# Final mLSTM states and forget gates moved in whole rows, and a chunk's decay weights made by one addition and four exponentials, in a one-layer hybrid encoder kernel

## The chip, the cores and the metric

The kernel runs on one core of a Trainium2 chip, in one launch. The metric is the time of the program on the device in microseconds; the time before is the median of three runs. A profiled execution is a run of its own and has its own time. TensorE, VectorE (DVE), ScalarE (ACT), GpSimd (POOL) and SyncE (SP) are the engines; each takes its instructions in the order in which they were laid down, and SP issues nearly all DMAs.

## The reference

One layer is computed for 1024 prompt rows and 32 sample rows with the same weights (D_MODEL 1024). A projection w_in feeds three groups of heads, w_o joins them, and a gated feed-forward network follows; LayerNorms stand between. Cut to what matters here:

```python
# mLSTM, 4 heads of 64 (the kernel: 8 prompt chunks of 128 rows, 1 sample chunk of 32)
dmat    = where(causal, bT[t] - bT[s] + li[s], -inf)
m       = max(m0 + bT, max_s dmat)                 # running stabiliser
s       = (q k^T) * exp(dmat - m)                  # the chunk's weights
num     = s v + (q C0) * exp(m0 + bT - m)
den     = max(|s.sum + (q n0) * exp(m0 + bT - m)|, exp(-m))
h       = num / den
C1, n1  = d0 * C0 + w_end k v^T,  d0 * n0 + w_end k
hm      = head_norm(h) * g * sigmoid(o_gate)
# FoX: 8 heads, causal softmax(q k^T / 8 + F[t] - F[s]) v,  F = cumsum(logf)
# gMLP: LayerNorm, then a causal 128x128 mix of rows per group
mix = concat(hm, hf, hg) @ w_o ;  x = LN(...) ;  y = silu(h w_gate) * (h w_up) @ w_down ;  x = LN(...)
```

Outputs beside y are the keys, values and log forget gates of FoX, the mLSTM states C, n and m of both row groups, and a normalised gMLP value.

## The kernel before, in words

**Layout.** All matrix products are of fp32 numbers split in two fp32r parts, three matmuls each (L118, L119, L120; the row-wise projections L283 to L285, named `tm`). 9060 matmul instructions go out on TensorE. The split is made on the way: ACT casts the high part (L106), DVE or POOL subtracts the low part (L107).

**Stages.** The projections come first (`fm`, `tm`), then attention heads and mLSTM chunks mixed into the rest of the projections and into the feed-forward network of the first row group (`up`, `dn`). ORDER (L42) is a string of units: `q` and `g` make operands, `f` emits a FoX head, `a` a slice of the adaLN product, `m0` to `m3` the first four mLSTM chunks. Chunks 4 to 8 are emitted by `mixers()`, woven with FoX heads 1 to 5. Emission order is not the order on the engines: the framework's scheduler simulates time and places the instructions, with a priority lead (HPA = 200) for FoX and mLSTM. Any change of a buffer or a duration can so move instructions of other parts.

**One chunk** (`mlstm(j)`): loads of q and k (tag `mqk`), of q in block form (`mqb`), v (`mv1`), the output gate (`mo`, L608), the row of maxima (`mb`). ACT makes the sigmoid of `mo` in three passes (L613 to L615). Then the weights `mw`: four DVE instructions (L622), one per head, each max(mb − col, maskbig), and one ACT Exp over all four heads (L624). TensorE multiplies q and k (L627), DVE multiplies the weights in (L629), TensorE multiplies by v (L643) and the old state by q (L648), and DVE adds up `mtot` (L649, L651). L658 and L665 update the state `C`; `C` keeps a head's n as a 65th column beside its 64 columns. The head norm follows (L678 to L696), then `to_mix`: two transposes on TensorE (L706), a copy by ACT (L708) into `mixs` and a store to `dmix` in DRAM.

**Where it is read.** `wo_mix` loads `dmix` back, splits it (L1008/L1009 into `ah`, `al` for the first row group, L1016/L1017 for the second) and the w_o product starts. A gMLP tile has its own way there (`tm_gms`, L740), and FoX heads theirs: scores `fox_s` (L789), maxima on DVE (L793, L796), Exp on ACT (`fox_p`, L798), transposes (`fox_t`, L825), split (`fox_pth` L830 on ACT, `fox_ptl` L831 on DVE), product with v (`fox_o`, L833/L838) and a sum (`fox_fo`, L845). `dn_t` (L933) is a product with ones that gives a LayerNorm's pivot; POOL subtracts it in L1066.

**Buffers.** The tags of the mLSTM pool have one buffer each. `gates()` and the chunks share tags.

Of the kernel before, what the change touches and what calls it, by code (L numbers as in the profile page):

```python
# [15 lines left out]
P = 128  # L16
# [4 lines left out]
NS = 32  # L21
# [48 lines left out]
class Kernel:  # L70
# [365 lines left out]
    def gates(self):  # L436
        self.phase = "gates"
        nc, d = self.nc, self.d
# [24 lines left out]
        scan = t([R, 2, 192], "mqb")  # L463
        nc.gpsimd.memset(scan[:, :, 0:64], NEG)
        scan = [scan[:, 0], scan[:, 1]]
        fk = t([64, 4, P], "mqk", F32R)
        nc.gpsimd.memset(f(fk[:, 2:4, :]), 1.0)
        fq = t([64, 2, P], "mkw", F32R)
        rows4 = t([72, 4, P], "mb")
# [7 lines left out]
        ls, x = x[:, :, 16:28], x[:, :, 0:16]  # L477
        nc.vector.tensor_tensor(x, self.G, self.rowp[:, 0:16].unsqueeze(1).to_broadcast([P, 9, 16]), ALU.add)
        z = x[:, :, 4:16]
        a, e, s, s2 = (y[:, i] for y in (t([P, 2, 9, 12], x) for x in ("mtot", "mhm")) for i in range(2))  # L480
        p = t([P, 9, 12], "msq")
        nc.vector.scalar_tensor_tensor(a, z, -1.0, z, ALU.mult, ALU.min)
        nc.scalar.activation(e, a, AF.Exp)
        nc.vector.tensor_scalar(s, e, 2.0, None, ALU.add)
# [4 lines left out]
        for q in (15, 13, 11, 9, 7, 5, 3):  # L489
# [1 line left out]
        nc.vector.scalar_tensor_tensor(p, p, 1.0, s, ALU.add, ALU.mult)  # L491
        nc.vector.tensor_scalar(a, z, 0.0, None, ALU.min)
        nc.vector.scalar_tensor_tensor(ls, p, -2.0, a, ALU.mult, ALU.add)
        w = t([P, 180], "mixs", F32, 1)
        gi, gm, gn, gf = (w[:, o:o + 9 * n].rearrange("p (j h) -> p j h", h=n)
                          for o, n in ((0, 4), (36, 4), (72, 4), (108, 8)))
        nc.vector.tensor_copy(gf, ls[:, :, 4:12])
        nc.vector.tensor_copy(gi, x[:, :, 0:4])
# [64 lines left out]
        nc.vector.tensor_copy(self.col, ps[:, :4 * R].rearrange("p (g j h) -> p j g h", g=4, h=4))  # L563
        nc.scalar.activation(self.col[:, :, 1:4, :], self.col[:, :, 1:4, :], AF.Exp)
        yield
        self.store(d["o_lf"].rearrange("(j p) h -> p j h", p=P), ls[:, 0:8, 4:12])
        self.store(d["o_lfs"], ls[:NS, 8, 4:12])
        self.store(self.dM, M)
        self.store(d["o_m"], m0[:, 8:9])
        self.store(d["o_ms"], mes)  # L570
# [3 lines left out]
    def mlstm_states(self):  # L574
        nc, d = self.nc, self.d
        self.C = self.t(self.cst, [P, 2, 130], F32, "C")
        self.Cs = self.t(self.cst, [P, 2, 130], F32, "Cs")
        for x in (self.C, self.Cs):
            nc.gpsimd.memset(x, 0.0)
        for i in range(2):  # L580
            r = slice(64 * i, 64 * i + 64)
            self.load(self.Cs[r, :, 65 * i:65 * i + 64], d["state_C"][r])
            self.load(self.Cs[r, :, 65 * i + 64:65 * i + 65], d["state_n"][r].unsqueeze(2))
        self.d0c = self.t(self.cst, [P, 2, 9], F32, "d0c")
        for i in range(2):
            src = self.dd0.rearrange("(a two) j -> two a j", two=2)[i]
            self.load(self.d0c[64 * i:64 * i + 64], src.partition_broadcast(64))
        nc.scalar.activation(self.d0c, self.d0c, AF.Exp)

    def mlstm(self, j):  # L590
# [3 lines left out]
        C = self.C if j < 8 else self.Cs  # L594
        o = j * P
        t = lambda shape, tag, bufs=1: self.t(mx, shape, F32, tag, bufs)
        qk = t([P, 4, P], "mqk", 1)
        self.load(qk[:, :, :L], self.dmqk[:, :, o:o + L])
        qb = t([P, 2, 2, P], "mqb")
        nc.gpsimd.memset(qb, 0.0)  # L600
# [17 lines left out]
        self.phase = "mlstm"  # L618

        w = t([P, 4, P], "mw")  # L620
        for h in range(4):
            nc.vector.scalar_tensor_tensor(w[:L, h, :L], mb[:L, h, :L], col[:L, 0, h:h + 1],  # L622
                                           self.maskbig[:L, :L], ALU.subtract, ALU.max)
        nc.scalar.activation(w[:L, :, :L], w[:L, :, :L], AF.Exp, scale=-1.0)  # L624
        st = self.t(self.pss, [P, 512], F32, "s")
        for i in range(2):
            nc.tensor.matmul(st[:L, 256 * i:256 * i + 256].rearrange("p (a q) -> p a q", a=2)[:, :, :L],  # L627
# [38 lines left out]
                else:  # L666
                    nc.vector.tensor_copy(C[r, i, q], s)
        if j >= 7:
            oc, on = ("o_C", "o_n") if j == 7 else ("o_Cs", "o_ns")
            for a in range(2):  # L670
                r = slice(64 * a, 64 * a + 64)
                self.store(self.d[oc][r], C[r, :, 65 * a:65 * a + 64])
                self.store(self.d[on][r].unsqueeze(2), C[r, :, 65 * a + 64:65 * a + 65])
        yield
        self.phase = "mlstm"

# [8 lines left out]
        nc.vector.tensor_reduce(mu[:L], hm[:L], AX.X, ALU.add)  # L685
        nc.vector.tensor_scalar(mu[:L], mu[:L], 1.0 / 64, None, ALU.mult)
        nc.vector.tensor_tensor(hm[:L], hm[:L], bc(mu), ALU.subtract)
        sq = t([P, 4, 64], "msq")
        nc.scalar.activation(sq[:L], hm[:L], AF.Square)
        var = t([P, 4], "mvar")  # L690
        nc.vector.tensor_reduce(var[:L], sq[:L], AX.X, ALU.add)
# [9 lines left out]
    def to_mix(self, x, j, L, k0, pool, bank=None):  # L701

        nc = self.nc
        ps = bank or self.t(self.pt, [P, 512], F32, "t")
        for i in range(2):
            nc.tensor.transpose(ps[:, i * P:i * P + L], x[:L, i * P:(i + 1) * P], self.ident[:L, :L])  # L706
        s = self.t(pool, [P, 2, P], F32, "mixs", 1)
        nc.scalar.copy(s[:, :, :L], ps[:, :256].rearrange("p (i q) -> p i q", i=2)[:, :, :L])  # L708
        c = min(j // 4, 1)
        o = j * P - GO[c]  # L710
        self.store(self.dmix[c][:, k0:k0 + 2, o:o + L], s[:, :, :L])
# [876 lines left out]
def build(tc, d):  # L1588
# [4 lines left out]

_OUTS = {
    "o_yT": (8, 128, 1056), "o_kT": (8, 64, 1056), "o_v": (1024, 512), "o_vs": (32, 512),
    "o_lf": (1024, 8), "o_lfs": (32, 8), "o_C": (128, 2, 64), "o_n": (128, 2), "o_m": (4, 1),
    "o_Cs": (128, 2, 64), "o_ns": (128, 2), "o_ms": (4, 1), "o_vn": (32, 256),
}


def _layout(inputs):
    import numpy as np

    g = {k: np.asarray(v) for k, v in inputs.items()}
# [31 lines left out]
    qk = np.stack([fq.reshape(1024, 8, 64), fk.reshape(1024, 8, 64)], axis=2).reshape(1024, 1024)  # L1636
    a["w_in"] = units(np.concatenate([mq, mv, mo, gv, gu], axis=1), 256)
    a["w_in_f"] = units(np.concatenate([mk, qk], axis=1), 128)
    a["w_o"] = units(g["w_o"][0], 128)
    a["w_gu"] = np.concatenate([units(g["w_gate"][0], 128), units(g["w_up"][0], 128)], axis=-1)  # L1640
    a["w_dn"] = units(g["w_down"][0], 256)
    a["wsT"] = g["gmlp_ws"][0].transpose(2, 0, 1)
    a["cache_k"] = g["cache_fox_k"][0, 0].transpose(2, 1, 0)
    a["cache_v"] = g["cache_fox_v"][0, 0].reshape(2, 128, 512).transpose(1, 0, 2)
    a["cache_lf"] = g["cache_fox_logf"][0, 0].reshape(2, 128, 8).transpose(1, 0, 2)
    a["state_C"] = g["state_mlstm_C"][0, 0].reshape(2, 128, 64).transpose(1, 0, 2)
    a["state_n"] = g["state_mlstm_n"][0, 0].reshape(2, 128).T
    a["state_m"] = g["state_mlstm_m"][0, 0].reshape(4, 1)
    return {k: np.ascontiguousarray(v) for k, v in a.items()}


def _collect(r):
    import numpy as np

    y = r["o_yT"].reshape(1024, 1056).T
    k = r["o_kT"].transpose(2, 0, 1)
    v = r["o_v"].reshape(1, 1, 1024, 8, 64)

    def state(C, n, m):
        return (C.transpose(1, 0, 2).reshape(1, 1, 4, 64, 64), n.T.reshape(1, 1, 4, 64), m.reshape(1, 1, 4))  # L1660

    out = (y[None, :1024], y[None, 1024:], k[None, None, :1024], v, r["o_lf"].reshape(1, 1, 1024, 8),
           *state(r["o_C"], r["o_n"], r["o_m"]),
           k[None, None, 1024:], r["o_vs"].reshape(1, 1, 32, 8, 64), r["o_lfs"].reshape(1, 1, 32, 8),
           *state(r["o_Cs"], r["o_ns"], r["o_ms"]), r["o_vn"].reshape(1, 1, 32, 256))
    return tuple(np.ascontiguousarray(z) for z in out)


# [20 lines left out]
```

## Time and profile before

| | us |
|---|---|
| median of 3 runs | 1373.39 (1373.31 to 1374.2) |
| profiled execution | 1378.6, span 1376.5 |
| TensorE busy | 1335.4 (97%) |
| TensorE weight loads | 1215.7 (88%) |
| DVE busy | 998.5 (73%) |
| ACT busy | 653.3 (47%) |
| POOL busy | 225.2 (16%) |
| mean granted TensorE clock | 0.995 |

"Idle" of TensorE is time in which no matmul ran; a row of waits gives an engine and a line, what it waited for, the sum, the number of times and the longest. A row of the timeline gives start and duration, the engine and the line, the operation, and in brackets how long the engine stood before it and for whom. In the windows each engine's busy time stands in its column, with the granted clock, the DMA share and GB/s at the end.

### The profile page before, as it was taken

The page shows a single profiled execution, that of the slowest core. Times are in us where ns is not written, and L with a number is a line of the kernel's source. Part 1 is how long each engine was busy: PE and PEld are TensorE (multiplying, and loading weights), DVE is VectorE, ACT ScalarE, POOL GpSimd, SP SyncE. Part 2 cuts the span into 40 slices and gives each one's busy share as a digit, 9 for nine tenths or more (in the row PEclk, how much of TensorE's full clock was granted, in tenths as well). Part 3 has the DMA queues.
Part 4 walks back from the last instruction along what each step waited for, and adds up shares of the span by engine and source line. Part 5 has one row for each costly group of instructions (what it writes and reads, how often), then busy time and mean ns, then how long its engine had stood idle before and what let it go on. Part 6 is the DMA issues. An engine that isn't in the chain of part 4 may idle for free.

```text
span 1376.5 us, 25170 instructions
## 1 busy us (share of the span) xinstructions
PE 1335.4 (97%) x9434; PEld 1215.7 (88%) x9434; DVE 998.5 (73%) x2156; ACT 653.3 (47%) x1282; POOL 225.2 (16%) x259
## 2 busy tenths in 40 slices
PE   7999999999999999999999999999999999999996
PEld 4898889888899768888887889899999999999995
DVE  5545553688769557777766767778898988888777
ACT  3314444444536544545454355436564554545354
POOL 0202000043243200000000000374610000000341
PEclk9999999999999999999999999999999999999998
DMA  9765565545734765543444353564587768454321
GB/s 359 252 241 151 158 198 154 162 146 173 230 114 147 204 176 162 137 143 110 140 128 87 101 120 97 189 169 126 173 226 194 201 161 223 132 175 126 96 87 65
DMA packets 121450, 221.50 MB, mean 161 GB/s; under 512 B 21133, under 2 KB 64537, under 8 KB 121329
## 3 DMA queue, kind: packets, MB, share of 16 engines
q1 hardware_dynamic: 114000, 207.34, 49.0%
q0 software_dynamic: 5968, 11.80, 5.0%
q8 instruction: 74, 1.21, 0.4%
q10 hardware_dynamic: 1360, 0.76, 0.2%
q14 instruction: 48, 0.39, 0.1%
HBM read 188.07 MB, written 51.72 MB: 174 GB/s over the span
## 4 chain that ended last, share of the span: by engine, by line
PE 63%; DMA 5%; DVE 5%; ACT 1%; issue 1%; SPq 0%; ACTq 0%; DVEq 0%
PE up_g L118 5%; PE up_g L120 5%; PE up_g L119 5%; PE dn_g L118 4%; PE dn_g L120 4%; PE dn_g L119 4%; PE sup_u L120 3%; PE sup_u L118 3%; PE sup_u L119 3%; PE sup_g L119 2%; PE sup_g L120 2%; PE sup_g L118 2%; PE wo_g L118 2%; PE dn_u L118 2%; PE wo_g L120 2%; PE dn_u L119 2%
## 5 line engine op out<-in xcount | busy, mean ns | idle before, releaser
L118 PE MATMUL up_g<-mlstm_ah,up_whi 128*128 128x512 f32 (+1 forms) x384 | 141.3, 368 | 2.4 <-DVE up_sil L1147 1.4
L120 PE MATMUL up_g<-mlstm_ah,up_wlo 128*128 128x512 f32 (+1 forms) x384 | 140.6, 366 | 0.0
L119 PE MATMUL up_g<-mlstm_al,up_whi 128*128 128x512 f32 (+1 forms) x384 | 140.5, 366 | 0.0
L1216 ACT CAST sup_whi<-sup_raw 128x1024 fp32r<-128x1024 f32 x54 | 56.0, 1048 | 90.1 <-PE dn_u L119 46.0
L118 PEld LDWEIGHTS up_g<-mlstm_ah,up_whi 128*128 128x128 f32 x384 | 72.6, 189 | 14.6 <-DVE up_sil L1147 1.6
L120 PEld LDWEIGHTS up_g<-mlstm_ah,up_wlo 128*128 128x128 f32 x384 | 72.6, 189 | 11.4
L107 DVE TENSOR_TENSOR up_wlo<-up_raw,up_whi 128x1024 fp32r<-128x1024 f32 x50 | 65.0, 1301 | 23.8 <-ACT up_whi L106 23.3
L106 ACT CAST up_whi<-up_raw 128x1024 fp32r<-128x1024 f32 x50 | 52.4, 1048 | 62.9 <-PE up_g L119 17.5
L119 PEld LDWEIGHTS up_g<-mlstm_al,up_whi 128*128 128x128 f32 x384 | 72.6, 189 | 10.8
L798 ACT ACTIVATE fox_p<-fox_s,fox_fmx 128x384 f32<-128x384 f32 (+2 forms) x96 | 55.2, 579 | 47.0 <-DVE fox_fmx L796 37.2
L1217 DVE TENSOR_TENSOR sup_wlo<-sup_raw,sup_whi 128x1024 fp32r<-128x1024 f32 x54 | 68.0, 1263 | 10.7 <-ACT sup_whi L1216 10.7
L120 PE MATMUL dn_g<-up_acth,dn_wlo 128*128 128x512 f32 (+2 forms) x200 | 73.6, 368 | 0.0
L119 PE MATMUL dn_g<-up_actl,dn_whi 128*128 128x512 f32 (+2 forms) x200 | 73.4, 368 | 0.0
L118 PE MATMUL dn_g<-up_acth,dn_whi 128*128 128x512 f32 (+2 forms) x200 | 73.4, 368 | 0.0
L1071 DVE SCALAR_TENSOR_TENSOR wo_z<-dn_g,start_mod,wo_z 128x512 f32<-128x512 f32 (+4 forms) x120 | 60.3, 521 | 13.4 <-PE dn_g L120 13.0
L106 ACT CAST dn_whi<-dn_raw 128x1024 fp32r<-128x1024 f32 (+1 forms) x44 | 42.7, 971 | 49.9 <-PE dn_u L119 11.1
L830 ACT CAST fox_pth<-fox_t 128x512 fp32r<-128x512 f32 (+1 forms) x80 | 41.0, 544 | 51.9 <-PE fox_t L825 51.8
L831 DVE TENSOR_TENSOR fox_ptl<-fox_t,fox_pth 128x512 fp32r<-128x512 f32 (+1 forms) x80 | 49.5, 631 | 16.7 <-ACT fox_pth L830 16.5
L107 DVE TENSOR_TENSOR dn_wlo<-dn_raw,dn_whi 128x1024 fp32r<-128x1024 f32 (+1 forms) x44 | 49.5, 1126 | 15.8 <-ACT dn_whi L106 15.5
L793 DVE TENSOR_REDUCE fox_fmx<-fox_s 128x1 f32<-128x384 f32 (+2 forms) x96 | 52.7, 553 | 10.1 <-PE fox_s L790 9.1
L283 PE MATMUL tm_g<-tm_whi,start_ah 128*128 128x256 f32 (+1 forms) x192 | 55.1, 290 | 0.0
L283 PE MATMUL tm_g<-tm_whi,start_h1h 128*128 128x256 f32 (+1 forms) x192 | 54.8, 286 | 0.3 <-DVE tm_traw L353 0.2
(668 smaller groups left out, 4813.3 us busy)
## 6 DMA issues: line engine op xcount, KB each, us to landing
up_raw<-w_gu SPq DMA_DIRECT2D x50, 512.0 KB
dn_raw<-w_dn SPq DMA_DIRECT2D x28, 512.0 KB
ada_late<-w_ada SPq DMA_DIRECT2D x24, 512.0 KB
sup_raw<-w_gu SPq DMA_DIRECT2D x20, 512.0 KB
start_dp<-w_gu SPq DMA_DIRECT2D x19, 512.0 KB
start_dp<-w_gu POOLq DMA_DIRECT2D x19, 512.0 KB, 7.5
wo_raw<-w_o SPq DMA_DIRECT2D x18, 512.0 KB
sup_raw<-start_dp SPq DMA_DIRECT2D x18, 512.0 KB
```

The source lines that it names most:

```text
L106: nc.scalar.copy(hi[:, :w], raw[:, :w])
L107: (eng or nc.vector).tensor_tensor(lo[:, :w], raw[:, :w], f(hi[:, :w]), ALU.subtract)
L118: nc.tensor.matmul(ps, hi, xh(k), start=start and k == 0, stop=False)
L119: nc.tensor.matmul(ps, hi, xl(k), start=False, stop=False)
L120: nc.tensor.matmul(ps, lo, xh(k), start=False, stop=stop and k == n - 1)
L283: nc.tensor.matmul(ps[:, :ncol], xh, hi, start=k == 0, stop=False)
L793: nc.vector.tensor_reduce(mxs[:, x:x + 1], s[:, :w], AX.X, ALU.max, negate=True)
L798: nc.scalar.activation(pr[:, lo:hi], banks[x][:, :hi - lo], AF.Exp, bias=mxs[:, 0:1], accum_out=sums[:, x:x + 1])
L831: nc.vector.tensor_tensor(pl[:, :e], ps[:, :e], f(ph[:, :e]), ALU.subtract)
L1071: self.lastz = self.nc.vector.scalar_tensor_tensor(z[:, m, x:y], ps[:, x - a:y - a], g[i], z[:, m, x:y], ALU.mult, ALU.add)
L1216: nc.scalar.copy(h, x)
L1217: tt(l, x, f(h), ALU.subtract)
```

## The change

Four edits. (1) The final states `o_C` and `o_n` (and `o_Cs`, `o_ns`) leave in one store each of the whole state tile, 128 rows of 260 floats, in place of four stores (two of 64-float pieces, two of single floats). The initial state comes in by one such load, so its tile is no longer zeroed by POOL. The host cuts the blocks out. (2) The log forget gates leave as one store of 72 floats a row from the tile `gw`, in place of two stores of 8-float pieces. (3) A chunk's weights: one DVE addition mb + maskbig of 128x512 (L617 after), and four ACT Exps of 128x128 with col as the bias (L620 after). (4) `mqk` has two buffers. For the room, tag `msq` and tag `mixs` are dropped: the squares of the head norm and the result of `to_mix` now lie in `mtot`, and temporaries of `gates()` in other tags. So the next chunk's `mtot` waits until the store to `dmix` has read it. The counts: DVE 2158 to 2131 instructions, ACT 1199 to 1226, POOL 264 to 263, SP 712 to 702, TensorE as before.

```diff
-        fk = t([64, 4, P], "mqk", F32R)
+        fk = t([64, 4, P], "mqk", F32R, 2)
...
-        a, e, s, s2 = (y[:, i] for y in (t([P, 2, 9, 12], x) for x in ("mtot", "mhm")) for i in range(2))
-        p = t([P, 9, 12], "msq")
+        y = t([P, 4, 9, 12], "p", F32, 4)
+        a, e, s, s2 = (y[:, i] for i in range(4))
+        p = t([P, 9, 12], "mtot")
...
-        self.store(d["o_lf"].rearrange("(j p) h -> p j h", p=P), ls[:, 0:8, 4:12])
-        self.store(d["o_lfs"], ls[:NS, 8, 4:12])
+        self.store(d["o_lf"], gw[:, 108:180])
...
-        for x in (self.C, self.Cs):
-            nc.gpsimd.memset(x, 0.0)
-        for i in range(2):
-            r = slice(64 * i, 64 * i + 64)
-            self.load(self.Cs[r, :, 65 * i:65 * i + 64], d["state_C"][r])
-            self.load(self.Cs[r, :, 65 * i + 64:65 * i + 65], d["state_n"][r].unsqueeze(2))
+        nc.gpsimd.memset(self.C, 0.0)
+        self.load(self.Cs, d["state_C"])
...
-        qk = t([P, 4, P], "mqk", 1)
+        qk = t([P, 4, P], "mqk", 2)
...
+        nc.vector.tensor_tensor(w[:L, :, :L], mb[:L, :, :L],
+                                self.maskbig[:L, :L].unsqueeze(1).to_broadcast([L, 4, L]), ALU.add)
         for h in range(4):
-            nc.vector.scalar_tensor_tensor(w[:L, h, :L], mb[:L, h, :L], col[:L, 0, h:h + 1],
-                                           self.maskbig[:L, :L], ALU.subtract, ALU.max)
-        nc.scalar.activation(w[:L, :, :L], w[:L, :, :L], AF.Exp, scale=-1.0)
+            nc.scalar.activation(w[:L, h, :L], w[:L, h, :L], AF.Exp, bias=col[:L, 0, h:h + 1], scale=-1.0)
...
         if j >= 7:
-            oc, on = ("o_C", "o_n") if j == 7 else ("o_Cs", "o_ns")
-            for a in range(2):
-                r = slice(64 * a, 64 * a + 64)
-                self.store(self.d[oc][r], C[r, :, 65 * a:65 * a + 64])
-                self.store(self.d[on][r].unsqueeze(2), C[r, :, 65 * a + 64:65 * a + 65])
+            self.store(self.d["o_C" if j == 7 else "o_Cs"], C)
...
-        sq = t([P, 4, 64], "msq")
+        sq = t([P, 4, 64], "mtot")
...
-        s = self.t(pool, [P, 2, P], F32, "mixs", 1)
+        s = self.t(pool, [P, 2, P], F32, "mtot", 1)
```

How the order moves on the engines is shown at three places. Line numbers after the change are 4 less at the weights' product (L625 for L629) and 4 to 8 less behind it.

First SP where chunk 7 ends and chunk 8's output gate is loaded, before:

```order
454 L87 DMA mlstm_mv_1392_7233<-start_dmv_61 32x4x64
455 L91 DMA o_C<-fm_C_2249 128x1x64
456 L91 DMA o_n<-fm_C_2249 128x1x1
457 L91 DMA o_C<-fm_C_2249 128x1x64
458 L91 DMA o_n<-fm_C_2249 128x1x1
459 L87 DMA mlstm_mo_7236<-start_dmo_62 32x256
460 L87 DMA dn_raw_9490<-w_dn 128x1024
461 L87 DMA fox_v_7199<-start_dv_59 128x8x128
```

and after:

```order
451 L87 DMA dn_raw_9410<-w_dn 128x1024
452 L91 DMA o_C<-fm_C_2247 128x260
453 L87 DMA mlstm_mo_7227<-start_dmo_62 32x256
454 L87 DMA dn_raw_9444<-w_dn 128x1024
455 L87 DMA fox_v_7190<-start_dv_59 128x8x128
456 L91 DMA start_dmix_33_89<-mlstm_mtot_7183 128x2x128
```

The load of `mo` still follows the state store directly; four rows became one.

Second DVE between the last step of chunk 1 (`mhm` times `mo`) and the `mtot` of chunk 2, before:

```order
455 L665 SCALAR_TENSOR_TENSOR fm_C_2249<-fm_C_2249,fm_d0c_2257,mlstm_s_3539 64x65 x4
456 L696 TENSOR_TENSOR mlstm_mhm_3550<-mlstm_mhm_3550,mlstm_mo_3505 128x256
457 L733 SCALAR_TENSOR_TENSOR tm_vhl_4136<-tm_g_4111,start_colp_108,tm_vhl_4136 128x2x64 x4
458 L629 TENSOR_TENSOR mlstm_mw_3646<-mlstm_s_3652,mlstm_mw_3646 128x512
459 L637 TENSOR_TENSOR mlstm_mkw_3659<-mlstm_t_3656,start_col_178 128x256
460 L622 SCALAR_TENSOR_TENSOR mlstm_mw_3829<-mlstm_mb_3823,start_col_178,start_maskbig_136 128x128 x4
461 L649 TENSOR_TENSOR mlstm_mtot_3666<-mlstm_s_3667,start_col_178 128x260
```

and after:

```order
456 L688 TENSOR_TENSOR mlstm_mhm_3544<-mlstm_mhm_3544,mlstm_mo_3499 128x256
457 L661 SCALAR_TENSOR_TENSOR fm_C_2247<-fm_C_2247,fm_d0c_2251,mlstm_s_3533 64x65 x4
458 L625 TENSOR_TENSOR mlstm_mw_3640<-mlstm_s_3646,mlstm_mw_3640 128x512
459 L633 TENSOR_TENSOR mlstm_mkw_3653<-mlstm_t_3650,start_col_178 128x256
460 L725 SCALAR_TENSOR_TENSOR tm_vhl_4130<-tm_g_4105,start_colp_108,tm_vhl_4130 128x2x64 x4
461 L617 TENSOR_TENSOR mlstm_mw_3823<-mlstm_mb_3817,start_maskbig_136 128x512
462 L645 TENSOR_TENSOR mlstm_mtot_3660<-mlstm_s_3661,start_col_178 128x260
```

The four subtractions (L622) are one addition (L617), and the state update moved behind the last step of chunk 1. L645 now needs the store of chunk 1's result, which is made from that last step.

Third TensorE where the last FoX head of the second row group ends, before:

```order
4907 L838 MATMUL fox_o_7778<-fox_pth_7822,fox_v_7653 128x256
4908 L833 MATMUL fox_o_7778<-fox_ptl_7823,fox_v_7653 64x256
4909 L838 MATMUL fox_o_7778<-fox_pth_7822,fox_v_7653 128x256
4910 L933 MATMUL dn_t_9926<-wo_z_755_3920,start_ones_45_140 128x512
4911 L119 MATMUL dn_g_10038<-up_actl_9559,dn_whi_10019 128x512
4912 L120 MATMUL dn_g_10038<-up_acth_9558,dn_wlo_10020 128x512
```

and after:

```order
4872 L830 MATMUL fox_o_7766<-fox_pth_7797,fox_v_7641 128x256
4873 L925 MATMUL dn_t_9914<-wo_z_754_3914,start_ones_45_140 128x512
4874 L825 MATMUL fox_o_7766<-fox_ptl_7811,fox_v_7641 64x256
4875 L830 MATMUL fox_o_7766<-fox_pth_7810,fox_v_7641 128x256
4876 L825 MATMUL fox_o_7766<-fox_ptl_7811,fox_v_7641 64x256
4877 L830 MATMUL fox_o_7766<-fox_pth_7810,fox_v_7641 128x256
4878 L119 MATMUL dn_g_9975<-up_actl_9691,dn_whi_9971 128x512
```

The end of the head and the pivot stand some 35 rows earlier. Up to the first w_o product of the second row group (row 5015 before, 5012 after) follow 8 rows of `dn_g` and 96 of `up` before, and 38 of `dn_g` and 96 of `up` after.

More of the change, by code (lines that the diff above doesn't have):

```diff
@@ L493, in gates @@
         nc.vector.scalar_tensor_tensor(ls, p, -2.0, a, ALU.mult, ALU.add)
-        w = t([P, 180], "mixs", F32, 1)
-        gi, gm, gn, gf = (w[:, o:o + 9 * n].rearrange("p (j h) -> p j h", h=n)
+        gw = t([P, 180], "mhm")
+        gi, gm, gn, gf = (gw[:, o:o + 9 * n].rearrange("p (j h) -> p j h", h=n)
                           for o, n in ((0, 4), (36, 4), (72, 4), (108, 8)))
@@ L1595 @@
     "o_yT": (8, 128, 1056), "o_kT": (8, 64, 1056), "o_v": (1024, 512), "o_vs": (32, 512),
-    "o_lf": (1024, 8), "o_lfs": (32, 8), "o_C": (128, 2, 64), "o_n": (128, 2), "o_m": (4, 1),
-    "o_Cs": (128, 2, 64), "o_ns": (128, 2), "o_ms": (4, 1), "o_vn": (32, 256),
+    "o_lf": (128, 72), "o_C": (128, 2, 130), "o_m": (4, 1),
+    "o_Cs": (128, 2, 130), "o_ms": (4, 1), "o_vn": (32, 256),
 }
@@ L1645, in _layout @@
     a["cache_lf"] = g["cache_fox_logf"][0, 0].reshape(2, 128, 8).transpose(1, 0, 2)
-    a["state_C"] = g["state_mlstm_C"][0, 0].reshape(2, 128, 64).transpose(1, 0, 2)
-    a["state_n"] = g["state_mlstm_n"][0, 0].reshape(2, 128).T
+    cn = np.concatenate([g["state_mlstm_C"][0, 0], g["state_mlstm_n"][0, 0][:, :, None]], axis=2)
+    cn = cn.reshape(2, 2, 64, 65).transpose(1, 2, 0, 3)
+    a["state_C"] = np.zeros((128, 2, 130), cn.dtype)
+    for i in range(2):
+        a["state_C"][64 * i:64 * i + 64, :, 65 * i:65 * i + 65] = cn[i]
     a["state_m"] = g["state_mlstm_m"][0, 0].reshape(4, 1)
@@ L1657, in _collect, with state @@
     v = r["o_v"].reshape(1, 1, 1024, 8, 64)
[L1659 to L1665, printed above, removed]
+    def state(C, m):
+        C = np.stack([C[64 * i:64 * i + 64, :, 65 * i:65 * i + 65] for i in range(2)])
+        C = C.transpose(2, 0, 1, 3).reshape(1, 1, 4, 64, 65)
+        return C[..., :64], C[..., 64], m.reshape(1, 1, 4)
+    lf = r["o_lf"].reshape(128, 9, 8).transpose(1, 0, 2)
+    out = (y[None, :1024], y[None, 1024:], k[None, None, :1024], v, lf[None, None, :8].reshape(1, 1, 1024, 8),
+           *state(r["o_C"], r["o_m"]),
+           k[None, None, 1024:], r["o_vs"].reshape(1, 1, 32, 8, 64), lf[8, :32].reshape(1, 1, 32, 8),
+           *state(r["o_Cs"], r["o_ms"]), r["o_vn"].reshape(1, 1, 32, 256))
     return tuple(np.ascontiguousarray(z) for z in out)
```

## The prediction

> **What bounds the kernel now.** I read the page first, then the stretches of 100 us, then what TensorE waited for, then the timeline of the other engines at each of its larger gaps.
>
> ```profile
> span 1376.5 us, 25170 instructions
> PE 1335.4 (97%) x9434; PEld 1215.7 (88%) x9434; DVE 998.5 (73%) x2156; ACT 653.3 (47%) x1282; POOL 225.2 (16%) x259
> ```
>
> TensorE works 1335.4 of 1376.5 us. The change takes no matmul away, so all it can win is in the 41 us of idle time and in time at a lower clock. Some of it is the start and the tail of the kernel. Within, the waits of TensorE show where it lies (total, times, longest):
>
> ```profile
> PE fox_s L789 <- ACT fox_p L798: 4.0, 3, 2.4
> PE wo_g L118 <- ACT up_ah L1016: 2.6, 1, 2.6
> PE fm_g L118 <- ACT tm_gms L740: 2.4, 1, 2.4
> PE mlstm_t L635 <- DVE fox_ptl L831: 2.3, 1, 2.3
> ```
>
> They are gaps of 2.3 to 2.6 us (fox_s has two small ones beside), and each lies where mLSTM chunks, attention heads or the operand of w_o pass from engine to engine. I take them one by one. Everything below is in time of the profiled execution.
>
> **The state stores (gap at 743 us).** The last chunk (j = 8) stands here; SP first stores the final state, then loads that chunk's output gates (mo). Timeline of SP, of ACT and of PE, then the chain of waits, then two stretches of 1 us (the last two columns are DMA share and GB/s):
>
> ```profile
> 728.33 0.60 SPq L91 DMA_DIRECT2D o_n<-fm_C  x1
> ...
> 731.93 0.34 SPq L87 DMA_DIRECT2D mlstm_mo<-start_dmo  x1
> 734.83 0.59 SPq L87 DMA_DIRECT2D fox_v<-start_dv  x1
> 740.59 0.41 ACT L613 ACTIVATE mlstm_mo<-mlstm_mo 32x256 f32<-32x256 f32 x1 [6.62 <-DMA mlstm_mo<-start_dmo]
> 743.07 0.44 PE L789 MATMUL fox_s<-fox_k,fox_qp 128*128 128x384 f32 x1 [2.36 <-ACT fox_p L798]
> 731.93 8.57 DMA mlstm_mo<-start_dmo
> 738.00:739.00 1.00, 1.00 (x6) 0.82 (x5) 0.00 (x0) 0.00 (x0) 0.00 (x0) 1.00 0.67 29
> 742.00:743.00 1.00, 0.00 (x0) 0.00 (x0) 0.57 (x2) 0.97 (x4) 0.00 (x0) 1.00 0.95 334
> ```
>
> A load of 32 KB takes 8.57 us, since almost nothing moves (29 GB/s at 738) until 742, although SP has issued a load of fox_v as well at 734.83. ACT stands in order behind that load at L613 for 6.62 us, fox_p L798 stands behind L613, and TensorE runs dry for 2.36 us. After such a gap the granted clock falls (windows of PE; third figure from the right):
>
> ```profile
> 744.00:746.00 2.00, 2.00 (x8) 0.58 0.50 143
> 746.00:748.00 2.00, 2.00 (x7) 0.56 0.34 37
> ```
>
> That is 2 × 0.42 + 2 × 0.44 = 1.7 us of lost work. The change writes the state as 128 rows of 1,040 B in place of 256 pieces of 256 B and 256 of 4 B, in one DMA instead of four. The price of the new store is not in the trace; its nearest row is the store of a chunk's result, 2.87 us (row below). If mo then lands 2.9 to 3.9 us after its issue at 731.93 (the rows of other transfers below), it is there at 735.8 at the latest, ACT loses at most 1.8 us instead of 6.62, and the 2.36 us are more than covered. **Term: 2.36 + 1.7 = 4.1 us gained**; bounds 0 (the stall is not of the stores) and 4.1. The stores of the last state (o_Cs, o_ns) appear in no wait of TensorE, so they gain nothing. Row then rule: the row above has 8.57 us behind 4 B pieces; the Trainium skill, page "DMA: Bandwidth & Descriptors", section "Specifications", sets 512 B as the least transfer at line rate, with a read-modify-write below that, which points the same way. But its section "Why small descriptors are slow (HBM only)" prices a packet at a fixed 3 cycles or so, and by that alone 512 small pieces would be no stall of microseconds and the term would be 0.
>
> The state loads at the start have the same form; I count nothing for them, since the waits above show no TensorE wait on them.
>
> **The weights of a chunk (gap at 303 us).** Durations of the forms (min/median/max in ns): old subtraction, old Exp, and for what is new the nearest forms, a DVE TENSOR_TENSOR of 128x512 (L629) and an ACT pass of 128x128 (mean in the last place but one):
>
> ```profile
> L622 DVE SCALAR_TENSOR_TENSOR mlstm_mw<-mlstm_mb,start_col,start_maskbig x36: 233/347/3212, 177.8 to 720.6; 128x128 f32<-128x128 f32 x32, 32x32 f32<-32x32 f32 x4
> L624 ACT ACTIVATE mlstm_mw<-mlstm_mw x9: 304/634/647, 178.9 to 721.2; 128x512 f32<-128x512 f32 x8, 32x128 f32<-32x128 f32 x1
> L629 DVE TENSOR_TENSOR mlstm_mw<-mlstm_s,mlstm_mw x9: 270/692/694, 252.1 to 753.5; 128x512 f32<-128x512 f32 x8, 32x128 f32<-32x128 f32 x1
> L798 ACT ACTIVATE fox_p<-fox_s,fox_fmx 128x128 f32<-128x128 f32 x8 | 2.9, 368 | 2.7 <-DVE fox_fmx L793 2.4
> ```
>
> DVE: 4 × 0.347 − 0.692 = 0.70 us less a chunk. ACT: 4 × 0.368 − 0.634 = 0.84 us more. Nine times each, 6 us and 8 us, on engines at 73% and 47%: off the path, except where they set a gap. That is here:
>
> ```profile
> 297.54 4.00 DVE L622 SCALAR_TENSOR_TENSOR mlstm_mw<-mlstm_mb,start_col,start_maskbig 128x128 f32<-128x128 f32 x4
> 297.51 2.40 POOL L107 TENSOR_TENSOR tm_wlo<-tm_raw,tm_whi 128x1024 fp32r<-128x1024 f32 x1
> 301.63 0.63 ACT L624 ACTIVATE mlstm_mw<-mlstm_mw 128x512 f32<-128x512 f32 x1 [3.44 <-DVE mlstm_mw L622]
> 303.45 0.44 PE L635 MATMUL mlstm_t<-start_ident,mlstm_mqk 128*128 128x128 f32 x2 [2.27 <-DVE fox_ptl L831]
> ```
>
> The first of the four subtractions stood behind POOL (its maximum of 3,212 ns), then ACT's Exp, then fox_pth, then fox_ptl, then TensorE. In the new order the one addition stands at the same place behind POOL, with two inputs in SBUF as well. It ends some 0.4 us sooner after the wait, and ACT gives that back with three more Exps ahead of fox_pth. **Term: 0**, bounds −4.0 (the 2.27 us go, and 1.7 us of clock as at 743) and +0.8.
>
> **Order: buffers and the wait that is added.** With two mqk buffers the attention and mLSTM stream stands 20 to 30 TensorE rows earlier. In exchange chunk j+1's tot (L649) shares its one buffer with chunk j's result and must wait for that store to land. DVE waits in order, with fox_ptl, the maxima of fox and the norms of gMLP queued behind it, and TensorE waits for those. Rows at chunk 1 to 2 and chunk 2 to 3, and the landing:
>
> ```profile
> 313.37 0.37 SPq L91 DMA_DIRECT2D start_dmix<-mlstm_mixs  x1
> 314.83 2.06 SPq L87 DMA_DIRECT2D mlstm_mqb<-start_dmqk  x2
> 320.17 0.42 DVE L649 TENSOR_TENSOR mlstm_mtot<-mlstm_s,start_col 128x260 f32<-128x260 f32 x1
> 340.84 0.97 DVE L696 TENSOR_TENSOR mlstm_mhm<-mlstm_mhm,mlstm_mo 128x256 f32<-128x256 f32 x1
> 344.42 0.37 SPq L91 DMA_DIRECT2D start_dmix<-mlstm_mixs  x1
> 357.84 2.87 DMA start_dmix<-mlstm_mixs
> 361.11 3.90 DMA mlstm_al<-start_dmix
> ```
>
> Chunk 1 to 2: the store could land at 313.37 + 2.87 = 316.2, 3.9 us ahead of L649. Now the two mqb loads go ahead of it on SP, so 314.83 + 2.06 + 2.87 + 0.4 = 320.2: it lands as L649 had begun. The wait eats what DVE saves and no more. Chunk 2 to 3: from L696's end (341.81) to the landing (344.42 + 2.87 = 347.29) are 5.5 us. Between these two steps on DVE stand about 6 us of work in the new order. No wait, by a margin of half a microsecond. **Term: 0**, with a bound of 2 us of DVE wait at each place if the store lands 4 us after issue and not 2.87.
>
> The last rows above are also the chain of the gap at 366: m3's store 2.87, the load of al 3.90, two ACT steps, TensorE. In the new order 13 instead of 8 tm matmuls stand between m3's transposes and the work that runs dry, and the chain has for one of them:
>
> ```profile
> 357.06 0.12 PE tm_g L284
> ```
>
> **Term: 5 × 0.12 = 0.6 us gained** of 2.4.
>
> The gap of 2.6 us ahead of wo_g (timelines of DVE and POOL, then two rows of the chain):
>
> ```profile
> 877.94 5.86 DVE L1017 TENSOR_TENSOR up_al<-wo_tmp,up_ah 128x272 fp32r<-128x272 f32 x4
> 873.88 11.06 POOL L1066 TENSOR_TENSOR wo_z<-wo_z,up_pv 128x512 f32<-128x512 f32 x7 [129.30 <-ACT up_pv L934]
> 885.47 1.49 DVE L1017 TENSOR_TENSOR up_al<-wo_tmp,up_ah 128x272 fp32r<-128x272 f32 x4
> 886.61 5.10 DMA wo_tmp<-start_dmix
> 873.18 0.23 PE dn_g L119
> ```
>
> L1017's four take 5.86 us beside POOL's pass against 1.49 us once POOL is done, so the last wo_tmp loads go out late. The last fox_o and the pivot that starts POOL (dn_t) now have 38 instead of 8 dn_g matmuls behind them before w_o: 30 × 0.23 = 7 us more, well over the 2.6. But DVE and SP have their own order there. **Term: 2.0 us gained**, bounds 0 and 2.6.
>
> **Sum.** 4.1 + 0.6 + 2.0 = 6.7 us: 1378.6 − 6.7 = 1371.9 for the profiled execution, whose span is 1376.5. The median of the runs shown is 1373.39, 5.2 us under it; the same difference makes **1366.7 us**.
>
> One rule on the clock bears on the spread. After the gaps of 2.27 us (303) and 2.36 us (743) the clock fell, and after that of 2.4 us at 366 it stayed at 1.00:
>
> ```profile
> 304.00:306.00 2.00, 2.00 (x11) 0.50 0.79 173
> 368.00:370.00 2.00, 2.00 (x20) 1.00 1.06 409
> ```
>
> So length does not decide it here, and any gap that is moved can win or lose 1.7 us. The Trainium skill, page "TensorE: Matmul & The Clock Gate", section "What's actually happening", has a free-running activity window of some 3.4 us: by that, no gap here would be long enough for a full idle window, and the term at 743 would be 2.36 alone. The rows at 744 and 746 speak against that.
>
> **The rivals.** (1) Only the stall at 743 goes; what the order wins at 366 and 892 it loses elsewhere: 1373.39 − 4.1 = 1369.3. For it: 4.1 is the one term with a direct cause. (2) More goes: the 303 gap too (its DVE steps fall past POOL's), and all of 892: 4.1 + 4.0 + 0.6 + 2.6 = 11.3, so 1362.1. Against it: the addition still meets POOL in the order. (3) The change does not do what it says: the 4 B pieces are not what starves mo, or mo's buffer is free later anyway; then only the order's terms are left, 0 to 2.6, and 1371 to 1373.4. For it: no row shows a store of 1,040 B rows by itself. Against it: nothing else stands between o_n and the silence. (4) **Slower:** tot's wait decides. The store of chunk 1 and of chunk 2 lands 2 us after DVE is ready, at the place where DVE is fullest; TensorE runs dry 2 us each and loses 1.7 us of clock each: 7.4 lost, 4.1 gained, 1373.39 + 3.3 = 1376.7. It decides from a landing of some 3.5 us on at chunk 2. For it: al's 3.90 us on the same queue, and SP holds al loads ahead of that store. Against it: TensorE has work from gMLP that does not wait for fox.
>
> **How the numbers follow.** About 0.2% (2.7 us) is what a measurement of this kernel can tell from no change. Chances: forecast 0.42, (1) 0.20, (2) 0.08, (3) 0.13, (4) 0.17. Forecast, (1) and (2) are faster by more than 2.7 us, less 0.03 for a miss inside them: 0.67. Same: (3), those 0.03 and 0.03 of (4) where only one wait falls: 0.19. Slower: 0.14. The range goes from (2)'s 1362.1 to (4)'s 1376.7; most of the chance lies in 1362 to 1370.
>
> **What would show it.** Right: mo's DMA under 4 us, no silence of the DMA engines after o_C, no gap of PE L789 on fox_p near 740, clock 1.00 there; the wait of wo_g on up_ah gone or under 1 us; the wait on tm_gms near 1.8. Wrong: mo still at 8 us; DVE L649 (L645 after) waiting for a DMA of start_dmix; more than 42 us of TensorE idle, or clock windows of 0.5 to 0.8 in new places.

## The result, and the profile after

The changed kernel is faster by 0.2%: median 1372.99 us of 12 runs against 1376.34 of 12 runs of before on the same chips (the first three of these gave the 1373.39 of the table above), ratio 0.9978 with a 95% interval of 0.9968 to 0.9989, or 3.0 us (1.5 to 4.4). The forecast was 6.7 us (ratio 0.9951). The direction was right and the size was not: 3.0 of 6.7 us came. The profiled execution has 1375.06 us against 1378.6, its span 1373.0 against 1376.5.

The page after, two lines:

```profile
span 1373.0 us, 25163 instructions
PE 1332.9 (97%) x9434; PEld 1216.8 (89%) x9434; DVE 989.9 (72%) x2129; ACT 657.5 (48%) x1309; POOL 223.6 (16%) x258
```

TensorE is idle for 40.1 us where it was 41.1: hardly less. But the idle time has moved. Stretches of 100 us of the changed kernel (length, busy time of TensorE, clock, DMA share, GB/s):

```profile
300.00:400.00 100.00, 89.69 (x711) 0.97 0.58 189
700.00:800.00 100.00, 100.00 (x514) 1.00 0.39 117
800.00:900.00 100.00, 100.00 (x628) 1.00 0.41 131
```

and the same of before:

```profile
300.00:400.00 100.00, 93.42 (x753) 0.98 0.61 192
700.00:800.00 100.00, 97.64 (x495) 0.98 0.45 106
800.00:900.00 100.00, 97.44 (x606) 1.00 0.44 135
```

From 700 to 900 TensorE now never stops: 4.9 us of gaps and the low clock behind 743 are gone, as forecast. From 300 to 400 it has lost 3.7 us more. The waits of TensorE after name the losses:

```profile
PE tm_g L722 <- DMA tm_gvn<-start_dvn: 3.0, 1, 3.0
PE fm_g L118 <- ACT tm_gms L732: 3.0, 1, 3.0
PE mlstm_t L631 <- DVE fox_ptl L823: 2.3, 1, 2.3
PE foxs_s L882 <- DMA foxs_k<-start_dsf: 1.8, 1, 1.8
```

The second and third are the gaps of 366 and 303 of before. The first is new: a load of gMLP values from DRAM (tm_gvn) that TensorE needs for L722 (L730 before). The fourth, 0.2 before, was gone in a second execution of the changed kernel.

The two gaps that went. Chunk 8's output gate, SP then ACT of the changed kernel:

```profile
729.92 0.34 SPq L87 DMA_DIRECT2D mlstm_mo<-start_dmo  x1
731.96 0.42 ACT L609 ACTIVATE mlstm_mo<-mlstm_mo 32x256 f32<-32x256 f32 x1 [0.58 <-DMA mlstm_mo<-start_dmo]
```

The load takes 2.0 us where it took 8.57, and ACT stands 0.58 us for it where it stood 6.62. And the operand of the second w_o product, POOL's pivot and ACT's last cast before it:

```profile
865.85 9.03 POOL L1058 TENSOR_TENSOR wo_z<-wo_z,up_pv 128x512 f32<-128x512 f32 x6 [129.63 <-ACT up_pv L926]
889.90 1.64 ACT L1008 CAST up_ah<-wo_tmp 128x272 fp32r<-128x272 f32 x4 [0.67 <-DMA wo_tmp<-start_dmix]
```

POOL starts at 865.85 where it started at 873.88, and the w_o product waits for nothing.

### The profile page after: what moved, and what is told of

Its sections match the earlier page's. It is cut to its first block, busy times and chain, and to the rows that moved or that the text cites. A ratio compares the mean times of both kernels' runs of the same rounds, so it can differ in the third digit from the quotient of the medians.

```text
span 1373.0 us, 25163 instructions
## 1 busy us (share of the span) xinstructions
PE 1332.9 (97%) x9434; PEld 1216.8 (89%) x9434; DVE 989.9 (72%) x2129; ACT 657.5 (48%) x1309; POOL 223.6 (16%) x258
## 4 chain that ended last, share of the span: by engine, by line
PE 81%; DVE 7%; DMA 7%; ACT 2%; issue 2%; SPq 1%; ACTq 0%; DVEq 0%
PE up_g L118 5%; PE up_g L120 5%; PE up_g L119 5%; PE dn_g L118 4%; PE dn_g L120 4%; PE dn_g L119 4%; PE tm_g L284 3%; PE tm_g L283 3%; PE tm_g L285 3%; PE sup_u L120 3%; PE sup_u L118 3%; PE sup_u L119 3%; PE fox_t L817 2%; PE sup_g L119 2%; PE sup_g L120 2%; PE sup_g L118 2%
## 5 line engine op out<-in xcount | busy, mean ns | idle before, releaser
L284 PE MATMUL tm_g<-tm_wlo,start_h1h 128*128 128x256 f32 (+1 forms) x192 | 54.9, 286 | 0.9 <-DVE tm_wlo L107 0.9
```

The costliest lines, as they stand in the source:

```text
L284: nc.tensor.matmul(ps[:, :ncol], xh, lo, start=False, stop=False)
```

## The experiments

Twelve experiments follow, two of them the kernels before and after once more. Ratios are against runs of before on the same chip. A ratio is given where a kernel was timed several times; e6, e7, e9 and e10 are one profiled execution each. The store of the log gates (part 2) and the load of the initial state were not tried by themselves.

### Each part alone, and the change without its buffers (e1 to e4)

e1, the state stores alone:

```diff
-            oc, on = ("o_C", "o_n") if j == 7 else ("o_Cs", "o_ns")
-            for a in range(2): ...  # four stores
+            self.store(self.d["o_C" if j == 7 else "o_Cs"], C)
```

> Before with one edit: o_C/o_n and o_Cs/o_ns leave as one whole-row store each. TensorE's order is that of before, row for row. Theory (the pieces of 256 B and 4 B starve the load of mo): that load lands in under 4 us after its issue instead of 8.57, TensorE's gap of 2.36 us near 743 and the low clock behind it are gone, every other gap stays (303: 2.3, 366: 2.4, 892: 2.6); 4.1 us faster than before. Rival (the order of the changed kernel took that gap away, not the stores): the gap near 743 stays, 0 us.

Ratio 0.9983 (0.9970 to 0.9995), 2.3 us. The gap near 743 is gone:

```profile
734.98 0.33 SPq L87 DMA_DIRECT2D mlstm_mo<-start_dmo  x1
736.93 0.40 ACT L613 ACTIVATE mlstm_mo<-mlstm_mo 32x256 f32<-32x256 f32 x1
```

The load takes 1.95 us at the most. TensorE's order is that of before, so the stores did this and not the order. But the other gaps were not what they had been: the same order waited 1.53 us for tm_gvn (0 in the first profile of before) and 3.0 for tm_gms (2.4). The theory's 4.1 us did not come in full, though the interval (0.7 to 4.1 us) does not shut it out.

e2, two mqk buffers and the tags that make room (the lines of `gates()` are left out here):

```diff
-        qk = t([P, 4, P], "mqk", 1)
+        qk = t([P, 4, P], "mqk", 2)
...
-        sq = t([P, 4, 64], "msq")
+        sq = t([P, 4, 64], "mtot")
...
-        s = self.t(pool, [P, 2, P], F32, "mixs", 1)
+        s = self.t(pool, [P, 2, P], F32, "mtot", 1)
```

> Before with one edit: two mqk buffers and the tags that pay for them (msq, mixs into mtot; gates' temporaries moved). Theory (this part moved the instructions, and the loss between 303 and 376 us is its): a TensorE wait of about 3 us on tm_gvn near 312 and one of about 3 on tm_gms near 366-370, the gap near 743 stays at about 2.4; slower than before by 2 to 6 us. Rival (the weights edit moved the instructions): no wait on tm_gvn over 0.5 us, time within 1.5 us of before.

Ratio 0.9992 (0.9980 to 1.0004): no difference that can be told. No wait on tm_gvn. So the theory, that the loss belongs to this part, fell. Its order has a gap of its own, 3.95 us at 333 for fox_p, and a smaller one (1.30) at 740.

e3, the weights alone:

```diff
-        for h in range(4):
-            nc.vector.scalar_tensor_tensor(w[:L, h, :L], mb[:L, h, :L], col[:L, 0, h:h + 1], ..., ALU.subtract, ALU.max)
-        nc.scalar.activation(w[:L, :, :L], w[:L, :, :L], AF.Exp, scale=-1.0)
+        nc.vector.tensor_tensor(w[:L, :, :L], mb[:L, :, :L], ..., ALU.add)
+        for h in range(4):
+            nc.scalar.activation(w[:L, h, :L], w[:L, h, :L], AF.Exp, bias=col[:L, 0, h:h + 1], scale=-1.0)
```

> Before with one edit: a chunk's weights by one addition and four Exps. Theory (its cost is hidden, and the 303 gap stays, since the one addition waits for POOL like the first of four): the addition near 298 takes 3.4 to 3.7 us, the gap near 303 is 2.2 to 2.3, no wait on tm_gvn over 0.5 us; within 1.5 us of before. Rival (this edit brings the loss): a tm_gvn wait of about 3 us, slower by 2 to 6 us.

Ratio 0.9999 (0.9988 to 1.0010). The rival is right about the wait (1.89 us), but not about the time. The gap at 303 was 2.23 us behind an addition of 3.60, as the theory had it. No gap stood near 743, and larger ones than in before, 1.4 to 1.9 us, stood at 453, 492 and 518. So the gaps moved, and TensorE was idle no less in sum (42.8 us, 41.1 in before). The wait:

```profile
311.28 1.13 PE L730 MATMUL tm_g<-tm_gvn,start_wsp 128*128 128x128 f32 x8 [1.89 <-DMA tm_gvn<-start_dvn]
```

e4, the changed kernel without the buffers of e2 (the lines of e2 the other way round):

> The changed kernel with one mqk buffer and the old tags (parts 1 to 3 of the change alone). Theory (the loss between 303 and 376 comes with the buffers): no tm_gvn wait over 0.5 us, no gap near 743; 4 us faster than before, and 1 us or more faster than the changed kernel. Rival (the loss belongs to any new order): a gap of 2 to 3 us on tm_gvn or elsewhere in 300 to 380 in this order too, no faster than the changed kernel.

Ratio 0.9991 (0.9978 to 1.0005). The rival again: 1.96 us on tm_gvn, 2.69 ahead of the w_o product. No gap near 743.

What follows from the four: a wait of some 2 us on tm_gvn is there with the weights' edit (e3, e4) and is not there with the buffers alone (e2). The wait by itself does not prove it, since e1, in the order of before, had 1.53 us as well; what the edit changes is the order on SP, shown below. And the gap ahead of the second w_o product was 2.6 to 2.75 us in all four, so no part alone takes it away.

### Weights and buffers together (e5)

The diffs of e2 and e3, with the stores of before.

> Before with two edits together: the weights (one addition, four Exps) and the two mqk buffers with their tags; the state and gate stores are those of before. TensorE's order is then that of the changed kernel row for row, with the pivot dn_t 139 matmuls ahead of the second w_o product (105 in before and in either edit alone). Theory (the gap ahead of that product goes by this order): no wait of wo_g on up_ah near 890, where e1 to e4 all had 2.6 to 2.75 us; 2 to 4 us faster than before. Rival (the stores took it away): the gap stays at 2.6.

Ratio 0.9983 (0.9965 to 1.0001). The gap ahead of w_o is gone and the one near 743 is there (1.88 us). Only with both edits does the scheduler put the pivot early; the order alone does it, and the stores have no part in it. The time is 2.3 us under before, with an interval that just reaches no difference. The wait on tm_gvn is there too (1.69 us).

### Which pieces stop the DMAs (e6, e7)

e6 is e1 with the single floats stored as well:

```diff
             self.store(self.d["o_C" if j == 7 else "o_Cs"], C)
+            for a in range(2):
+                r = slice(64 * a, 64 * a + 64)
+                self.store(self.d["o_n" if j == 7 else "o_ns"][r].unsqueeze(2), C[r, :, 65 * a + 64:65 * a + 65])
```

> e1 with the old stores of single floats (o_n, o_ns) added behind the whole-row store, as outputs that nobody reads. TensorE's order is that of before. Theory (the 4 B pieces starve the load of mo): mo lands 7 us or more after its issue, ACT waits 4 us or more for it. Rival (the pieces of 256 B do it): mo lands about 2 us after its issue, as in e1.

e7 stores the state in pieces of 65 floats and no single ones:

```diff
-            self.store(self.d["o_C" if j == 7 else "o_Cs"], C)
+            for a in range(2):
+                r = slice(64 * a, 64 * a + 64)
+                self.store(self.d["o_C" if j == 7 else "o_Cs"][r], C[r, :, 65 * a:65 * a + 65])
```

> e1 with the state stored in two DMAs of 128 pieces of 260 B each (64 columns and n together), no single floats. TensorE's order is that of before. Theory (4 B pieces): mo lands about 2 to 3 us after its issue and ACT does not wait over 1 us for it. Rival (any piece under 512 B): mo lands after 5 us or more.

SP and ACT of e6:

```profile
731.93 0.33 SPq L87 DMA_DIRECT2D mlstm_mo<-start_dmo  x1
739.35 0.42 ACT L613 ACTIVATE mlstm_mo<-mlstm_mo 32x256 f32<-32x256 f32 x1 [5.39 <-DMA mlstm_mo<-start_dmo]
```

and of e7:

```profile
728.36 1.24 SPq L91 DMA_DIRECT2D o_C<-fm_C  x2
732.60 0.34 SPq L87 DMA_DIRECT2D mlstm_mo<-start_dmo  x1
734.53 0.40 ACT L613 ACTIVATE mlstm_mo<-mlstm_mo 32x256 f32<-32x256 f32 x1
```

7.42 us with the single floats, 1.93 us at the most without them. The pieces of 4 B stop the load, and pieces of 260 B do not. Of the rule that the Trainium skill gives on the page "DMA: Bandwidth & Descriptors", section "Specifications" (512 B as the least transfer at line rate), only this much shows here: 4 B were far too small, and 260 B were small enough to be under it and cost mo nothing.

### The gap at 303 (e8)

```diff
-GENG = (0, 1, 1, 0)
+GENG = (0, 0, 0, 0)
```

> The changed kernel with GENG = (0, 0, 0, 0): the low parts of the gMLP weights (four subtractions of 128x1024) on DVE and not on POOL. Theory (the gap near 303 is DVE's addition waiting for POOL's 2.4 us subtraction): the addition near 298 takes 0.7 to 1.5 us instead of 3.6, the gap near 303 falls from 2.25 to under 1, tm_gvn is loaded earlier; 1 to 4 us faster than the changed kernel. Rival (the added 4 x 1.2 us of DVE work in its fullest stretch eat it): the same wait elsewhere between 280 and 350, no faster than the changed kernel.

Ratio 0.9940 (0.9923 to 0.9958), median 1369.04: 8.3 us under before. The addition of the changed kernel, then that of e8 (DVE):

```profile
297.83 3.60 DVE L617 TENSOR_TENSOR mlstm_mw<-mlstm_mb,start_maskbig 128x512 f32<-128x512 f32 x1
295.35 0.88 DVE L617 TENSOR_TENSOR mlstm_mw<-mlstm_mb,start_maskbig 128x512 f32<-128x512 f32 x1
```

Without POOL's subtraction beside it the addition takes 0.88 us instead of 3.60, and the 303 gap and the wait on tm_gvn are both gone. The DVE work that is added shows only as waits of 0.6 to 0.8 us between 316 and 328; tm_gms is waited for once more, 2.93 us at 377.

### The same kernels again (e9, e10)

Before and the changed kernel, each unchanged, a second profiled execution.

> The kernel before, unchanged, a second profiled execution. Theory (the waits on loads between 300 and 380 differ from execution to execution, and the first profile of before had few of them): the gaps near 303 (2.3) and 743 (1 to 2.4, behind a load of mo of 7 us or more) and 890 (2.4 to 2.8) come again; a wait on tm_gvn of 0 to 1.6 us and one on tm_gms of 2 to 3; mean granted clock anywhere in 0.991 to 0.996. Rival (the profile repeats itself to 0.2 us): no wait on tm_gvn, 2.4 on tm_gms.

> The changed kernel, unchanged, a second profiled execution. Theory: the load of a fifth 512 KB piece (tm_raw) stands ahead of tm_gvn in SP's order whatever the execution: tm_gvn lands 9 us or more after its issue, TensorE waits 1.5 to 3 us for it near 311; no gap near 735 or 890; the wait on foxs_k near 484 is 0 to 1.8. Rival (the tm_gvn wait of 3 us was chance): under 0.7 us.

1377.8 us for before, 1371.66 for the changed kernel. In e9 the gap near 743 came again, but only 1.45 us of it, and with no low clock behind it. The clock fell behind 303, as in the first execution, and here also behind the gaps at 366 and 489. There was no wait on tm_gvn. Windows of 2 us:

```profile
304.00:306.00 2.00, 2.00 (x13) 0.63 0.99 295
744.00:746.00 2.00, 1.77 (x10) 1.00 0.58 169
```

In e10 the new wait came again, almost to the hundredth. Chain and TensorE, first of the changed kernel, then of e10:

```profile
303.32 9.15 DMA tm_gvn<-start_dvn
312.60 0.96 PE L722 MATMUL tm_g<-tm_gvn,start_wsp 128*128 128x128 f32 x6 [3.05 <-DMA tm_gvn<-start_dvn]
302.07 9.13 DMA tm_gvn<-start_dvn
311.33 1.62 PE L722 MATMUL tm_g<-tm_gvn,start_wsp 128*128 128x128 f32 x6 [3.03 <-DMA tm_gvn<-start_dvn]
```

So it belongs to the kernel. The wait on tm_gms was 2.32 in e9 and 2.97 in e10, as in the first profiles (2.43 and 2.96).

### The new wait taken away (e11, e12)

SP of the changed kernel shows what stands ahead of tm_gvn:

```profile
301.46 0.33 SPq L87 DMA_DIRECT2D mlstm_mb<-start_dM  x1
301.88 0.38 SPq L87 DMA_DIRECT2D tm_raw<-w_in  x1
302.36 0.86 SPq L87 DMA_DIRECT2D ada_late<-w_ada  x2
303.32 0.46 SPq L87 DMA_DIRECT2D tm_gvn<-start_dvn  x1
```

and of e9 (before again):

```profile
294.27 0.33 SPq L87 DMA_DIRECT2D tm_raw<-w_in  x1
300.31 0.33 SPq L87 DMA_DIRECT2D mlstm_mb<-start_dM  x1
300.74 0.86 SPq L87 DMA_DIRECT2D ada_late<-w_ada  x2
301.70 0.37 SPq L87 DMA_DIRECT2D tm_gvn<-start_dvn  x1
```

mb has one buffer, so chunk 3's can be loaded only when chunk 2's weights are made from the last one, and these stand behind POOL. In before tm_raw (512 KB) was ahead of mb on SP and so went out 6 us earlier. In the changed kernel it stands behind mb, goes out with the two loads of ada_late, and tm_gvn comes after 1.5 MB instead of 1 MB. The weights' edit brings this order: e3, e4 and e5 have it as well, e1, e2, e6 and e7 do not. From tm_gvn's issue to the first matmul that waited for it passed 9.3 to 9.5 us in the five profiles with the new order on SP (e3, e4, e5, the changed kernel, e10) and 7.4 to 7.7 us in the two of the old order in which TensorE waited for it at all (e1 1.53 us, e6 1.22). e11 gives mb a second buffer (and mqk one, for the room):

```diff
-        qk = t([P, 4, P], "mqk", 2)
+        qk = t([P, 4, P], "mqk", 1)
...
-        mb = t([P, 4, P], "mb", 1)
+        mb = t([P, 4, P], "mb", 2)
```

> The changed kernel with two buffers for mb (and one for mqk, since both do not fit): the load of the next chunk's mb no longer waits for the weights' addition, and the load of tm_raw no longer stands behind it on SP. Theory (the tm_gvn wait is that order on SP): tm_raw is issued some 5 us ahead of ada_late, tm_gvn lands 7.3 to 7.9 us after its issue as in before, the wait near 311 is under 1 us; pivot 139 matmuls ahead, so no gap near 890; 1 to 3 us faster than the changed kernel. Rival (the wait comes from TensorE's order): 1.5 us or more near 311.

Ratio 0.9938 (0.9919 to 0.9957), median 1370.01: 8.5 us under before by the ratio, where the changed kernel has 3.0. SP and TensorE of e11:

```profile
295.21 0.34 SPq L87 DMA_DIRECT2D tm_raw<-w_in  x1
298.66 0.92 SPq L87 DMA_DIRECT2D ada_late<-w_ada  x2
300.46 0.33 SPq L87 DMA_DIRECT2D tm_gvn<-start_dvn  x1
309.84 1.05 PE L722 MATMUL tm_g<-tm_gvn,start_wsp 128*128 128x128 f32 x8
```

tm_raw is early again, tm_gvn is not behind mb, and L722 does not wait. (When tm_gvn landed can't be read here, since nothing waited for it.) Over the changed kernel that is 5.5 us by the two ratios, where 1 to 3 were expected; by an estimate from their two intervals it may be 2.5 to 8.5. Its profile also has none of the low clock between 310 and 380 that both profiles of the changed kernel have. The one mqk buffer was not tried without the second mb, so its share is not known.

e12 is e11 with the GENG of e8.

> e11 with GENG = (0, 0, 0, 0), the gMLP weights' low parts on DVE. Theory (the two cures add up): no gap near 303 and none on tm_gvn over 0.7 us; as fast as e8 or faster, 7 to 10 us under before. Rival (e8 has no tm_gvn wait left to take away, and one mqk buffer costs): 1 to 3 us slower than e8.

Ratio 0.9943 (0.9923 to 0.9963), median 1368.68. As fast as e8 and e11 and no faster: the intervals lie on each other. This fits that both cures take away the same thing, the load of mb held up behind POOL. What the second removes besides (the 303 gap) came back in part as a wait of 1.66 us on the single mqk buffer at 307; the wait on tm_gms (3.38 us) was 3.29 in e11 already. e8, e11 and e12 all beat both kernels.

## Why the prediction was wrong in size

**The state stores: right, mis-sized.** The mechanism was as written: single floats, mo, ACT, TensorE (e1, e6, e7). The term of 4.1 us was 2.36 of gap and 1.7 of clock from one execution, and both were at their largest there, by luck. In three other executions with the old stores (e2, e5, e9) the gap was 1.30, 1.88 and 1.45 us, with no clock lost behind it; e3, in another order, had no gap there at all. e1 measures the whole term at 2.3 us (0.7 to 4.1). The rival by which only the order counts fell.

**The gap ahead of w_o: right.** 2.0 expected, 2.56 gone, by the order (e5), with POOL's pass earlier as the step had it.

**The weights at 303: right in its term. The order: this step failed.** The addition did wait like the first of the four subtractions (3.60 us), and the gap is 2.25 where it was 2.27. But the step "Order: buffers and the wait that is added" came to no loss. It looked at the new wait of mtot and at the mqb loads, and not at what else the new order did on SP: a 512 KB load (tm_raw) passed behind the load of mb. Its price is the missing term, 3.05 us at 312 (3.03 in e10, none in e11, where mb has a second buffer). Of it some 2.1 us are the later start of that product (312.60, L730 in before 310.54), and the rest is that TensorE came to it sooner. With it came the low clock there:

```profile
314.00:316.00 2.00, 2.00 (x11) 0.50 0.47 128
```

**The gap at 366: wrong.** 0.6 us was to be gained and 0.5 was lost. The step took the chain of m3 as standing still while TensorE got more to do. But the chain's store went out 3.0 us later (357.84 before), and its last load took longer (3.90 before):

```profile
360.87 2.94 DMA start_dmix<-mlstm_mtot
364.20 4.92 DMA mlstm_al<-start_dmix
```

Why it took longer stays open. Before's own order had this gap at 3.02 us in e1, so part of the loss may be of the execution.

**The wait of mtot (the slower rival): did not come.** In the changed kernel no DVE instruction waits for a store of start_dmix. DVE waited for TensorE at chunk 2, as in before.

**The account.** The same product of TensorE, an `up_g` that waits for ACT's start_qks, before and after:

```profile
450.72 0.38 PE L118 MATMUL up_g<-mlstm_ah,up_whi 128*128 128x256 f32 x1 [0.97 <-ACT start_qks L378]
455.99 0.39 PE L118 MATMUL up_g<-mlstm_ah,up_whi 128*128 128x256 f32 x1 [0.97 <-ACT start_qks L378]
```

At that place the changed kernel is 5.3 us late. It lost 3.05 for tm_gvn, 0.5 at 366, 0.4 by 303, 0.8 in small waits on DVE and ACT between 334 and 346, and 1.7 for one stretch of low clock more (behind 312 and 370, where before has one behind 303). Two small waits of before are gone, 0.5. That makes 6.0, and the 0.7 too much were not traced. From there on it wins 8.8 us and ends 3.5 earlier: 2.36 and 1.7 at 743, 2.56 ahead of w_o, 2.6 where fox_s no longer waits between 488 and 523 and 0.6 at 1002, less 1.5 on foxs_k. For the first half the forecast had a gain of 0.6. For the second it had 6.1, and the profile shows 6.6 in the same two places. The 2.6 of fox_s was in no term. It goes with the tags of part 4: TensorE's gaps between 484 and 532 come to 1.4 to 4.0 us in all seven profiles with the old tags (before, e9, e1, e3, e4, e6, e7), and to 0.3 at most in the seven with the new ones, the wait on foxs_k in the first profile of the changed kernel apart.

**The low clock.** The prediction was right that the length of a gap does not decide whether the clock falls. The traces show what does. In all of them the clock falls to 0.50 for 3.41 us at a time, a loss of 1.7 us, and within one execution the starts lie whole multiples of 3.41 us apart (in before 304.01 and 744.33, 129 times 3.413). Where these stretches lie against the kernel differs from execution to execution. Pairs of neighbouring stretches, in before those at 303 and at 366, then in the changed kernel those at 303 and at 312 (length, TensorE busy, clock, DMA share, GB/s):

```profile
300.60:304.01 3.41, 1.14 (x10) 1.00 0.40 74
304.01:307.42 3.41, 3.41 (x17) 0.50 0.83 237
362.04:365.45 3.41, 1.84 (x16) 1.00 0.78 224
365.45:368.86 3.41, 2.55 (x19) 1.00 1.04 396
299.67:303.08 3.41, 1.90 (x15) 1.00 0.10 33
303.08:306.49 3.41, 2.66 (x22) 1.00 0.95 273
309.91:313.32 3.41, 0.72 (x6) 1.00 1.05 368
313.32:316.73 3.41, 3.41 (x18) 0.50 0.57 145
```

A gap that lies in one stretch (2.27 us idle of 3.41, 2.69 of 3.41) is followed by a low one; a gap that a boundary cuts in two (1.57 and 0.86; 1.51 and 0.75) is not. In the fourteen traces, start and end of the kernel apart, every stretch with 1.8 us or more of idle time was followed by a low one and none with less than 1.6 was; in between both came. One case is outside this: in e1 the clock stayed low for three stretches, 10.2 us, behind the gap at 366, though the first two of them held only 0.84 and 0 us of idle time. So whether a gap of some 2.3 us costs 1.7 us more is chance, in the term at 743 as well. No run set the place of the stretches on purpose.

## What to carry to other kernels

When an edit moves instructions, read the DMA queue's own order first: a load that waits for a buffer holds back every load behind it. Here one large load slipped behind such a load, went out 6 us later together with the next ones, and cost a wait of 3 us, about what the best part won. A store made of single floats should be folded into a whole-row one even where nobody waits for it, since the next load does. And a term read from one profile is worth what a second execution leaves of it: the gap at 743 was 2.36 us in one and 1.45 in the next, and only the first lost clock behind it.

## What the runs showed of the hardware that was not expected

Two DMAs of 128 single floats each, issued by 729.62 us, kept a 32 KB load back until 740.5, and the same came in every run with such stores (6.1 to 8.7 us from mo's issue to ACT's start, in before, e2, e3, e5, e6 and e9); 256 pieces of 260 B kept back nothing (1.93 us in e7). The granted clock fell behind the gap of 303 in before (0.50) and not in the changed kernel, where the gap was as long, and the other way round at 366. What decided it was how much of the gap fell into one of the fixed stretches of 3.41 us: 2.27 us of idle time in one were enough, 1.57 were not.
